# The MLP's first token block: its operands made tile pair by tile pair, or first half before second half

## Chip, cores and metric

The kernel runs on one core of a Trainium2 chip. The metric is device time in microseconds: the median of three runs of the kernel before is 1969.99 us (1968.49 to 1970.82). A profile of one execution goes with it.

## The reference

One decoder layer on 2048 tokens of 1024 features, float32 throughout. A mixer block (attention with a window of 128 and a short gated convolution, joined by an output projection) is followed by the MLP:

```python
x = x + y @ w_out[l]
hm = rms_norm(x, mlp_norm_g[l])
x = x + jnp.square(jax.nn.relu(hm @ w_up[l])) @ w_down[l]
```

`w_up` is 1024 x 4096, `w_down` 4096 x 1024.

## The kernel before

Each float32 product is made as three fast matmuls, on the high and the low parts of both operands (an ACT cast gives the high part, a DVE subtraction the low one). The mixers go through four chunks of 512 tokens. The MLP's up projection goes over two token blocks of 1024 tokens, and in each it is a two by two block product done with seven instead of eight products: the activations of a token block are cut into four blocks (feature half by token half), called b11, b21 (first 512 tokens) and b12, b22 (other 512 tokens), and seven operands are made of them. Operand 1 is b11, 2 is b21, 3 is b22, and 5, 6, 7, 4 are differences. The products are taken in the order of `ORDER`, 1, 2, 6, 5, 3, 7, 4; the first eight of them use operands 1 and 2 alone, for four groups of columns each.

**Making the operands of the first token block** is the job of `prepare_mlp` (L887 on), and this is what the change touches. A residual stream `x1` lies in DRAM, token by token. A tile pair (jj, i) holds 128 features of each feature half, jj of 0 to 3, for 512 tokens, i of 0 (first half) or 1 (other half). One step of the loop does this:

- DVE transposes (L313) two 128 x 512 halves of a fetched tile into blocks of `xs`, and scales each in place (L314). That is `turned`, two calls.
- SP fetches the tile pair two steps ahead: `load_turned`, four pieces (L307). The fetched tiles `xt` have two buffers, so the fetch of step n + 2 waits for the transposes of step n.
- For i = 0, two stores put the blocks into the operands 1 and 2 in DRAM (`x_put`, L318).
- For i = 1, `x_sums` does four differences (L324) and five stores (L318), in this order:

```python
x_put(tb, jj, 3, b22)
sub(5, t1, b12, b11)
sub(6, b11, b22, t1)
sub(7, b12, b22, b12)
sub(4, b21, b21, b11)
```

Each `sub` is a DVE subtraction and a store of its result; the second and the fourth overwrite b11 and b21, which were stored as operands 1 and 2. The blocks lie in two tiles `xs` of eight blocks each, which take the place of the normed activations of the last chunk (tags `h0`, `h1`), so the loop can't begin before the last chunk's projections are done with these.

The loop is a generator. `besides` (L918 on) takes one of its steps, then three groups of matmuls of the output projection, and so on; the output projection of the last chunk has a conv half (matmuls on `yt_c`) and an attention half (on `at_b`), each over two halves of the columns, and its evictions run on DVE (L872). After the last step and the rest of the conv half, `begin_mlp` emits what the MLP needs first: `load_x(0, 1)`, that is two SP loads of operand 1 from DRAM (L379) with a cast on ACT (L380) and a subtraction on DVE (L381), then four pieces of up weights (`wu_first`, L391) with their casts (L396, L397). Behind it come the output projection's last weights (`w_wo`, L235), then operand 2 and the loop over the products (matmuls at L1404).

What sets the order: the framework fixes each engine's list of instructions when the program is built, from the order in which the code emits them, shifts of priority (`ahead`, `PRIO`; zero for this loop) and its own estimate of when inputs and buffers are free. On the chip each engine, and SP's queue of DMA issues too, runs its list in order and waits at semaphores.

Of the kernel before, what the change touches and what calls it, by code (L numbers as in the profile page):

```python
# [50 lines left out]
NB = BW // P  # L51
# [51 lines left out]
def hymba_layer(  # L103
# [53 lines left out]
    def row(tag, name, bufs, dt=F32):  # L157

        return pool.tile([P, D], dt, tag=tag, name=name, bufs=bufs)
# [35 lines left out]
    def ahead(i):  # L195

        offset = PRIO[stage[0]][i]
        return tc.high_priority(offset=offset) if offset else nullcontext()
# [103 lines left out]
    def load_turned(xb, src, r0, jj):  # L302

        for pg in range(4):
            rows = src[r0 : r0 + BW].rearrange("(q i) (k c) -> i k q c", i=TS, k=2)
            c0 = jj * P + pg * TS
            nc.sync.dma_start(  # L307
                xb[pg * TS : (pg + 1) * TS].rearrange("p (k q c) -> p k q c", k=2, c=TS), rows[:, :, :, c0 : c0 + TS]
            )

    def turned(xb, k, dst, g, rs_row):

        nc.vector.transpose(dst, xb[:, k * BW : (k + 1) * BW])  # L313
        nc.vector.scalar_tensor_tensor(dst, dst, g, rs_row, op0=ALU.mult, op1=ALU.mult)  # L314

    def x_put(tb, jj, i, b):

        nc.sync.dma_start(xop_dram[tb][ORDER.index(i)][:, jj * BW : (jj + 1) * BW], b)  # L318

    def x_sums(tb, jj, b11, b21, b12, b22, t1):  # L320


        def sub(i, dst, a, b):
            nc.vector.tensor_tensor(dst, a, b, op=ALU.subtract)  # L324
            x_put(tb, jj, i, dst)
# [6 lines that stand above are left out]
# [192 lines left out]
    with tc.tile_pool(name="mix_small", bufs=1) as mix_small, tc.tile_pool(name="mix", bufs=1) as mix:  # L524
# [362 lines left out]
        def prepare_mlp():  # L887


            xs = [pool.tile([P, 8, CH], F32, tag=f"h{i}", name=f"xm{i}", bufs=1) for i in range(2)]  # L890
            rows = pool.tile([P, 2, BW], F32, tag="gb", name="rs_rows", bufs=1)
            for i in range(2):
                nc.sync.dma_start(rows[:, i], rs_dram[i].partition_broadcast(P))
            xts = {}

            def fetch(jj, i):
                xts[jj, i] = row("xt", f"xt_m{i}_{jj}", 2)
                load_turned(xts[jj, i], x1_dram, i * BW, jj)

            tiles = [(jj, i) for jj in range(NB) for i in range(2)]  # L900
            fetch(*tiles[0])
            fetch(*tiles[1])
            yield
            for n, (jj, i) in enumerate(tiles):
                bs = [xs[jj % 2][:, m] for m in range(5)]
                with ahead(9):
                    for k in range(2):
                        turned(xts[jj, i], k, bs[2 * i + k], g_cols[:, NB * k + jj : NB * k + jj + 1], rows[:, i])
                if n + 2 < len(tiles):
                    fetch(*tiles[n + 2])  # L910
                if i:
                    x_sums(0, jj, *bs)
                else:
                    x_put(0, jj, 1, bs[0])
                    x_put(0, jj, 2, bs[1])
                yield

        def besides(c, before, h, yt, rc, x1, h_next, z_next):  # L918
# [12 lines left out]
            if c + 1 < NCHUNK:  # L931
                h_next += parts(pool, "h", f"h{c + 1}")
                steps = prepare(xf, (c + 1) * CH, g_row[0], h_next, f"a{c + 1}")
            else:
                steps = prepare_mlp()
# [615 lines left out]
```

## Time and profile before

| | |
|---|---|
| profiled execution | 1970.88 us |
| its span | 1969.2 us |
| median of three runs | 1969.99 us |
| PE busy | 1916.1 us, 97% |
| DVE busy | 1212.6 us, 62% |
| ACT busy | 827.1 us, 42% |
| POOL busy | 275.0 us, 14% |
| HBM read, written | 284.78 MB, 125.84 MB |

The profile shows one execution, in us from its start. PE is the matmul engine, DVE the vector engine, ACT the scalar engine, POOL GpSimd, SP the engine whose queue issues most DMAs (SPq in rows). A timeline row has the start, the length, the engine, the line of the kernel, the operation, the tiles written and read, how many such instructions were merged, and in brackets the engine's idle time before it and what ended that. The length of a merged row reaches from the first start to the last end. A row of the chain of waits has start, length and who held the end at that time. A row of the windows has a stretch, its length, and for each engine the busy time and the number of instructions.

### The profile page before, as it was taken

To read this page: it belongs to the slowest core of one execution; us is meant where nothing else is said; L and a number is where in the kernel's file an instruction comes from. 1 tells how busy PE (TensorE), PEld (TensorE's weight loads), DVE (VectorE), ACT (ScalarE), POOL (GpSimd) and SP (SyncE) were. 2 spreads that over 40 slices of the span, in tenths; PEclk is the share of its full clock that TensorE was granted. 3 is DMA by queue.
4 is the path that set the end of the run, shared out by engine and by line. 5 is a ranking of instruction groups with operands and counts; after the bars stand their busy time and mean duration, and the time that the engine had idled before them with its cause. 6 is when DMAs were issued, how large, how long until landed. Compare 5 with 4: busy or idle time off the path is not lost.

```text
span 1969.2 us, 24719 instructions
## 1 busy us (share of the span) xinstructions
PE 1916.1 (97%) x8961; PEld 1595.4 (81%) x8961; DVE 1212.6 (62%) x1896; ACT 827.1 (42%) x1577; POOL 275.0 (14%) x475
## 2 busy tenths in 40 slices
PE   9999999999999949999999999999999999999999
PEld 8888877888888737788887888888888888888887
DVE  4885656448456857789879767666544334447441
ACT  6564444335434216445456545554332233232320
POOL 1122212312221101322201111011000000100000
PEclk9999999999999969999999999999999999999999
DMA  9774864564674588877876444437964456766641
GB/s 321 276 271 128 267 246 171 203 225 155 198 256 171 145 266 289 207 221 234 246 232 217 161 165 145 150 123 259 392 236 149 143 163 228 257 233 214 214 141 54
DMA packets 269387, 412.26 MB, mean 209 GB/s; under 512 B 84936, under 2 KB 174032, under 8 KB 257488
## 3 DMA queue, kind: packets, MB, share of 16 engines
q1 hardware_dynamic: 240512, 335.15, 51.8%
q0 software_dynamic: 15488, 51.40, 7.1%
q10 hardware_dynamic: 13264, 24.13, 3.3%
q8 instruction: 71, 1.16, 0.2%
q14 instruction: 52, 0.43, 0.1%
HBM read 284.78 MB, written 125.84 MB: 209 GB/s over the span
## 4 chain that ended last, share of the span: by engine, by line
PE 84%; issue 5%; DMA 5%; DVE 3%; POOL 2%; ACT 1%; SPq 1%; POOLq 0%; DVEq 0%; ACTq 0%
PE d L1511 31%; PE u L1404 24%; PE pout L266 2%; PE pout L267 2%; PE pout L268 2%; PE pz L266 2%; PE pz L267 2%; PE pz L268 2%; PE pc_c L268 1%; PE px_c L266 1%; PE px_c L268 1%; PE px_c L267 1%; PE pc_c L266 1%; PE pc_c L267 1%; PE psc_b L645 1%
## 5 line engine op out<-in xcount | busy, mean ns | idle before, releaser
L1404 PE MATMUL u<-op_x,wop 128*128 128x512 f32 x2688 | 620.5, 393 | 38.9 <-ACT wop L396 34.7
L1404 PEld LDWEIGHTS u<-op_x,wop 128*128 128x128 f32 x2688 | 509.3, 190 | 149.6 <-ACT wop L396 35.6
L1511 PE MATMUL d<-op_w,op_f 128*128 128x512 f32 x2688 | 609.4, 389 | 0.0
L1511 PEld LDWEIGHTS d<-op_w,op_f 128*128 128x128 f32 x2688 | 504.7, 188 | 104.6
L381 DVE TENSOR_TENSOR op_f<-op_f 128x1024 fp32r<-128x1024 f32 x112 | 136.8, 1224 | 233.5 <-ACT op_f L380 233.3
L380 ACT CAST op_f<-op_f 128x1024 fp32r<-128x1024 f32 x112 | 117.5, 1051 | 355.2 <-DMA op_f<-fop 352.2
L396 ACT CAST wop<-wu 128x512 fp32r<-128x512 f32 x156 | 96.2, 620 | 97.7 <-PE u L1404 92.3
L397 DVE TENSOR_TENSOR wop<-wu,wop 128x512 fp32r<-128x512 f32 x156 | 111.1, 713 | 37.4 <-DMA wu<-in_w_up_dram 20.1
L1140 POOL DMA_DIRECT2D fop<-s x96 | 52.1, 543 | 442.4 <-DVE s L1143 435.4
L1146 DVE TENSOR_TENSOR u<-u,u 128x512 f32<-128x512 f32 x128 | 87.6, 684 | 23.2 <-PE u L1404 23.2
L381 DVE TENSOR_TENSOR op_w<-raw,op_w 128x1024 fp32r<-128x1024 f32 x56 | 68.3, 1222 | 26.6 <-ACT op_w L380 26.6
L380 ACT CAST op_w<-raw 128x1024 fp32r<-128x1024 f32 x56 | 58.8, 1052 | 43.7 <-PE d L1511 20.3
L1152 ACT ACTIVATE u<-u 128x512 f32<-128x512 f32 x64 | 40.5, 632 | 54.2 <-DVE u L1146 52.3
L662 ACT ACTIVATE sc_b<-sc_b,ngm_b 128x128 f32<-128x128 f32 x128 | 49.6, 389 | 27.3 <-DVE ngm_b L659 27.3
L380 ACT CAST op_x<-op_x 128x1024 fp32r<-128x1024 f32 x28 | 29.2, 1047 | 72.3 <-DMA op_x<-xop 72.2
L694 POOL TENSOR_SCALAR_AFFINE_SELECT pp_b<-pp_b 128x512 fp32r<-128x512 f32 x60 | 41.2, 698 | 104.3 <-ACT pp_b L687 47.9
L1353 POOL DMA_DIRECT2D wds<-raw x16 | 8.5, 534 | 333.8 <-DVE raw L1351 333.8
L396 ACT CAST wop<-wu_s 128x512 fp32r<-128x512 f32 x64 | 39.4, 620 | 37.4 <-PE u L1404 30.1
L266 PE MATMUL pout<-w_wo,yt_c 128*128 128x512 f32 x128 | 52.0, 406 | 0.0
L268 PE MATMUL pout<-w_wo,yt_c 128*128 128x512 f32 x128 | 51.4, 402 | 0.0
L267 PE MATMUL pout<-w_wo,yt_c 128*128 128x512 f32 x128 | 50.7, 396 | 0.0
L266 PE MATMUL pout<-w_wo,at_b 128*128 128x512 f32 x128 | 50.1, 394 | 0.2 <-DVE x L872 0.2
(252 smaller groups left out, 3129.4 us busy)
## 6 DMA issues: line engine op xcount, KB each, us to landing
op_f<-fop SPq DMA_DIRECT2D x112, 512.0 KB, 4.4
raw<-in_w_down_dram SPq DMA_DIRECT2D x72, 512.0 KB, 4.4
wu<-in_w_up_dram SPq DMA_DIRECT2D x128, 256.0 KB, 4.0
w_wo<-wo SPq DMA_DIRECT2D x24, 1024.0 KB, 7.0
fop<-s POOLq DMA_DIRECT2D x96, 256.0 KB, 2.6
fop<-u ACTq DMA_DIRECT2D x64, 256.0 KB, 2.7
op_x<-xop SPq DMA_DIRECT2D x28, 512.0 KB, 7.8
w_q<-qkv SPq DMA_DIRECT2D x24, 512.0 KB, 6.0
```

The costliest lines, as they stand in the source:

```text
L266: nc.tensor.matmul(ps, st(0), mv(0), start=first, stop=False)
L267: nc.tensor.matmul(ps, st(0), mv(1), start=False, stop=False)
L268: nc.tensor.matmul(ps, st(1), mv(0), start=False, stop=last)
L380: nc.scalar.copy(op[:, 0], raw)
L381: nc.vector.tensor_tensor(op[:, 1], raw, op[:, 0].bitcast(F32), op=ALU.subtract)
L396: splits.append(nc.scalar.copy(hi, blk).ins)
L397: nc.vector.tensor_tensor(lo, blk, hi.bitcast(F32), op=ALU.subtract)
L662: nc.scalar.activation(sc[:, hd, :], sc[:, hd, :], AF.Exp, bias=ngm[:, hd : hd + 1], accum_out=den[:, hd : hd + 1])
L1140: eng.dma_start(fop_dram[tb][ORDER_DOWN.index(i)][n // 2][:, n % 2], b)
L1146: return nc.vector.tensor_tensor(dst, ps, b, op=ALU.add).ins
L1404: nc.tensor.matmul(pt, wops[i][:, a, k, :], xops[tb, p][k // 2][:, b, k % 2, :], start=p not in GOES_ON and k + j == 0, stop=k + j == NB + ...
L1511: nc.tensor.matmul(ps[tb][j], fs[tb][:, a, k, j * P : (j + 1) * P], w[:, b, k, :], start=first and p not in GOES_ON and k + n == 0, stop=l ...
```

## The change

The loop takes all four tile pairs of the first 512 tokens and then all four of the other 512, in place of taking the two in turn for each jj. The blocks of the first half now stay until the second loop: all eight lie in the first tile of `xs`. The second half's two blocks and the scratch block `t1` lie in the second tile, in two sets of three that are used in turn. What a step computes, fetches and stores is the same, and so are all shapes.

```diff
-            tiles = [(jj, i) for jj in range(NB) for i in range(2)]
+            tiles = [(jj, i) for i in range(2) for jj in range(NB)]
             fetch(*tiles[0])
             fetch(*tiles[1])
             yield
             for n, (jj, i) in enumerate(tiles):
-                bs = [xs[jj % 2][:, m] for m in range(5)]
+                bs = [xs[0][:, 2 * jj + k] for k in range(2)]
+                if i:
+                    bs += [xs[1][:, 4 * (jj % 2) + k] for k in range(3)]
                 with ahead(9):
                     for k in range(2):
                         turned(xts[jj, i], k, bs[2 * i + k], g_cols[:, NB * k + jj : NB * k + jj + 1], rows[:, i])
                 if n + 2 < len(tiles):
                     fetch(*tiles[n + 2])
                 if i:
                     x_sums(0, jj, *bs)
                 else:
                     x_put(0, jj, 1, bs[0])
                     x_put(0, jj, 2, bs[1])
                 yield
```

## The prediction

> **What bounds the kernel now.** I read the page first, then the windows by stretch around the one dip in its PE row, then the timelines of PE, SP and DVE there, and last the chain of waits across it.
>
> ```profile
> span 1969.2 us, 24719 instructions
> PE 1916.1 (97%) x8961; PEld 1595.4 (81%) x8961; DVE 1212.6 (62%) x1896; ACT 827.1 (42%) x1577; POOL 275.0 (14%) x475
> ```
> ```profile
> 660.00:680.00 20.00, 19.92 (x93) 16.05 (x92) 14.49 (x28) 4.75 (x8) 3.27 (x6) 1.00 0.52 134
> 680.00:700.00 20.00, 6.02 (x28) 4.69 (x26) 16.87 (x28) 0.00 (x0) 0.80 (x2) 0.73 0.71 163
> 700.00:720.00 20.00, 2.48 (x6) 1.78 (x7) 9.88 (x15) 4.38 (x6) 0.00 (x0) 0.50 1.04 326
> ```
> ```profile
> 685.63 0.39 PE L268 MATMUL pout<-w_wo,at_b 128*128 128x512 f32 x1
> 717.52 5.89 PE L1404 MATMUL u<-op_x,wop 128*128 128x512 f32 x13 [31.50 <-ACT wop L396]
> ...
> 736.64 21.92 PE L1404 MATMUL u<-op_x,wop 128*128 128x512 f32 x96
> ```
>
> PE is busy for 1916.1 of 1969.2 us, so the end moves by what PE's idle time changes. Of the 53 us that are idle, 31.5 lie in one place: PE is full up to 680 (19.92 of 20 us), ends the output projection at 686.0, and starts the MLP at 717.52. The changed loop runs in just this place. (The columns after the length are PE, PEld, DVE, ACT, POOL, the granted clock, the DMA share and GB/s.)
>
> Who holds PE is in the chain of waits and in SP's queue:
>
> ```profile
> 707.68 0.32 SPq L318
> 708.00 0.05 issue
> 708.09 0.41 SPq L379
> 708.60 7.24 DMA op_x<-xop
> 715.90 0.70 ACT op_x L380
> 716.61 0.25 issue
> 716.85 0.62 ACT wop L396
> ```
> ```profile
> 649.62 5.03 SPq L307 DMA_DIRECT2D xt_m<-x_dram  x4
> 654.69 1.14 SPq L318 DMA_DIRECT2D xop<-xm  x2
> 655.92 3.84 SPq L307 DMA_DIRECT2D xt_m<-x_dram  x4
> 659.87 11.16 SPq L318 DMA_DIRECT2D xop<-xm  x5
> 671.32 3.23 SPq L307 DMA_DIRECT2D xt_m<-x_dram  x4
> 674.60 2.29 SPq L318 DMA_DIRECT2D xop<-xm  x2
> 682.44 2.71 SPq L307 DMA_DIRECT2D xt_m<-x_dram  x4
> 685.25 5.03 SPq L318 DMA_DIRECT2D xop<-xm  x5
> 690.32 3.46 SPq L307 DMA_DIRECT2D xt_m<-x_dram  x4
> 693.83 1.13 SPq L318 DMA_DIRECT2D xop<-xm  x2
> 695.06 3.82 SPq L307 DMA_DIRECT2D xt_m<-x_dram  x4
> 698.98 9.01 SPq L318 DMA_DIRECT2D xop<-xm  x12
> 708.09 0.92 SPq L379 DMA_DIRECT2D op_x<-xop  x2
> 709.11 3.16 SPq L391 DMA_DIRECT2D wu_first<-in_w_up_dram  x4
> 712.32 4.05 SPq L235 DMA_DIRECT2D w_wo<-wo  x2
> 716.47 1.06 SPq L379 DMA_DIRECT2D op_x<-xop  x2
> ```
>
> Read downwards, SP's rows are the loop: four pieces of a tile pair fetched (L307), then two stores of a first half or five of a second half (L318), and only after the last store, issued at 707.68, the two loads of operand 1 (L379). From there it is 708.09 to 717.52, 9.4 us of load, cast and weight cast, to PE's first matmul. So **PE restarts 9.8 us after SP issues the loop's last store**, and the question is whether that point moves, or whether the loads come away from behind it.
>
> **The change, part by part.** The eight steps (a step is one tile pair) are regrouped. Before, steps 1, 3, 5, 7 have 4 DVE instructions (two transposes, two scalings) and 2 stores, and steps 2, 4, 6, 8 have 8 and 5 (four differences more, with five stores). After, steps 1 to 4 are the small ones, 5 to 8 the large ones. Nothing is added or removed: 48 DVE instructions, 28 stores, 32 fetches, the same shapes.
>
> *The order in SP's queue.* Operand 1 reads only stores of small steps, so its data are in DRAM after step 4 now. It gains only if its loads stand earlier in SP's queue, and that order is fixed when the program is built. Here the trace speaks:
>
> ```profile
> 674.51 0.39 PE L268 MATMUL pout<-w_wo,yt_c 128*128 128x512 f32 x1
> ```
> ```profile
> 503.71 8.65 SPq L307 DMA_DIRECT2D xt_m<-x_dram  x6
> ```
>
> Loads are let past earlier ones where the queue has room: six pieces of the first two fetches went at 503.71, far ahead of loads that the code emits before them. Yet from 649.62 to 716.47 SP's order is exactly the code's. The last output weights (L235 at 712.32) have their place free once the projection's conv half ends at 674.51, and the first up weights (L391 at 709.11) read an input; neither went ahead of any of the 12 pieces and 21 stores issued from then to the loop's end. So the order takes SP as full over the whole loop, in which a fetch or a store was always waiting. After the change the same number of them waits, with 20 of the 28 stores in the last four steps, so there is even more to issue at the end. I take the order as the code's again: operand 1 last. Price of this part: 0.
>
> *The work in front of the gap.* Six differences leave the stretch in which PE is busy. They were hidden beside full PE (19.92 of 20), so taking them away wins 0.
>
> *The work in the gap.* This is where they go. DVE in the gap:
>
> ```profile
> 686.50:708.00 21.50, 16.68 (x26) 0.56 0.93 266
> ```
> ```profile
> 686.79 1.29 DVE L313 STREAM_TRANSPOSE xm<-xt_m 128x512 f32<-128x512 f32 x2
> ...
> 696.58 1.30 DVE L313 STREAM_TRANSPOSE xm<-xt_m 128x512 f32<-128x512 f32 x2 [2.15 <-DMA xt_m<-x_dram]
> ...
> 701.60 1.30 DVE L313 STREAM_TRANSPOSE xm<-xt_m 128x512 f32<-128x512 f32 x2 [1.22 <-DMA xt_m<-x_dram]
> ...
> 706.21 1.44 DVE L324 TENSOR_TENSOR xm<-xm 128x512 f32<-128x512 f32 x2 [0.68 <-DMA xop<-xm]
> ```
> ```profile
> xop<-xm SPq DMA_DIRECT2D x28, 256.0 KB, 3.5
> xt_m<-x_dram SPq DMA_DIRECT2D x24, 128.0 KB, 3.8
> ```
>
> Step 5 starts at 686.79 behind the projection's last eviction and will start there again. Before, 26 of the loop's instructions are left then (x26; 2 differences of step 4, then 4, 8, 4, 8), 16.68 us, 0.64 each; they end at 707.65 because DVE also waits 2.15 + 1.22 + 0.68 = 4.05 us. After, 32 are left: 6 x 0.64 = 3.9 us more work. The three waits are what pays for it. The first two are fetches that stood behind five stores in SP's queue (685.25 before 690.32); the third is a difference that overwrites a block whose store had just been issued, and those stores are four steps old now.
>
> I lay the last four steps out with 8 x 0.64 = 5.13 us each: step 5 at 686.8, 6 at 691.9, 7 at 697.1, 8 at 702.2.
> - Step 7's fetch is issued when step 5's transposes end (688.1), with only two stores ahead of it, takes 3.46 us of SP, and its last piece lands 3.8 us after its issue, near 694.7: in time.
> - Step 5's five stores follow from 691.6 at about 0.6 us each (the seven from 698.98 take some 4 us), to 694.6; then step 8's fetch, 3.82 us, to 698.4, landed near 701.3: in time.
> - **The added wait** is on blocks. The second tile's two blocks and the scratch block come from a set that returns after two steps, not four. Step 7 needs step 5's fourth store landed: issued near 693.4, 3.5 us, 696.9: just in time. Step 8 needs step 6's fourth store, issued behind step 8's own fetch near 700.2, landed 703.7, where DVE is there at 702.2: **1.5 us**. Behind the waiting transpose on DVE stand only this step's own instructions; the last stores wait for them, and PE for those.
>
> The end is then 702.2 + 1.5 + 5.13 = 708.8, against 707.65: **1.2 us later**. The 9.8 us behind it stay, as the same loads follow.
>
> The landing of a store is the softest figure. The Trainium skill, page "DMA: Bandwidth & Descriptors", section "Anatomy of one DMA", puts a transfer at about 2.0 us plus bytes over 436 GB/s, an estimate of 2.6 us for 256 KB; by it step 8 would wait 0.6 us and the sum would be 0.3 us. The row's 3.5 us is at a DMA share of 0.93, so I keep it.
>
> **The sum.** The profiled execution took 1970.88 us, 1.7 more than its span, and is 0.9 above the median of 1969.99. 1969.99 + 1.2 = **1971.2 us**. About 0.2%, 3.9 us, is what a measurement of this kernel can tell from no change.
>
> **Rivals.**
> *A, the forecast: the stores move, the loads don't.* The change does not do what it says in time. For it: SP's order above. 1971.2, within 1 us below and 2.5 above.
>
> *B, operand 1's loads go ahead of the differences' stores.* That needs a moment in which the build sees SP without a waiting fetch or store after step 4. Step 4's two stores would follow the fetch of 682.44 from 685.2 to 686.4 and land 3.5 us later, 689.9; plus 9.4 us, PE starts at 699.3, 18.2 us earlier. It has work: 8 products of 12 matmuls on operands 1 and 2 (96 in 21.92 us) and the projection's last 48 (10.9 us at the same pace), some 33 us, while the differences, held up by 9.2 us of loads (0.92 + 3.16 + 4.05 + 1.06), end near 717 and operand 6 is ready near 727. So nothing is given back: 1970.0 - 18.2 = 1951.8. If the loads pass only the last step's five stores (about 4 us), 1966. Against it: neither ready load did so before.
>
> The matmuls after the gap run slowly, 13 in 5.89 us where 96 take 21.92 us: 2.9 us, with the granted clock at 0.50 in the stretch before. The page "TensorE: Matmul & The Clock Gate" of the Trainium skill, Part 1, has the clock halved after an idle window of about 3.4 us; by that rule a shorter gap of 13 us still costs these 2.9 us, so B is not worth more than 18.2.
>
> *C, slower: reuse after two steps decides.* Place: the first transposes of steps 7 and 8. If a store takes the 7.24 us of the load at 708.60, behind a full queue, step 7 waits until 693.4 + 7.2 = 700.6, 3.5 us, and step 8 until 707.4, where DVE arrives at 705.7, 1.7 us; the end is 712.5, 4.9 us later: 1974.9. With a landing of L the end is 700.2 + L + 5.13, so it decides from 6.2 us on. If the 4.05 us of waits stay too (the fetches late all the same), 1978. For it: the DMA share of 0.93. Against it: stores landed in 3.5 us at that very share.
>
> **How the numbers follow.** A 0.55, B 0.20 (0.10 whole, 0.10 in part), C 0.25. A lies within 0.2%, B is faster by over 0.2% (its smallest form sits at 4 us), C slower. The range leaves out the whole of B and the far end of C, about 0.16: 1962 to 1977.5. A alone: 1970.2 to 1973.7.
>
> **What would show it.** Right: SP's rows show 4, 2 four times, then 4, 5, 4, 5, 5, 5, and L379 behind the last L318; DVE runs 32 loop instructions from about 686.8 with under 2 us of waits; the fetch waits of 2.15 and 1.22 us are gone; a wait <-DMA xop<-xm stands before a transpose of step 8; PE's gap is 32 to 34 us. Wrong: L379 or L391 between L318 rows (B), or waits of over 2 us before the transposes of steps 7 and 8, or a later start than 686.8 (C). A shift in how PE mixes projection and MLP matmuls from 717 to 760 would be an effect that I have at nothing; its cover is that everything behind the last store is the same list.

## The result and the profile after

The changed kernel takes 1970.74 us (median of 20 runs, 1965.71 to 1975.53), the kernel before 1969.58 us (20 runs beside them, 1965.45 to 1971.42). The ratio is 1.0009, with a 95% interval of 1.0001 to 1.0017: 1.8 us slower, between 0.2 and 3.3. That is within the 0.2% of the forecast, which had +1.2 us. The profiled execution took 1968.23 us.

First the page of the changed kernel, its span and busy times:

```profile
span 1966.4 us, 24724 instructions
PE 1913.4 (97%) x8961; PEld 1592.7 (81%) x8961; DVE 1212.2 (62%) x1896; ACT 826.9 (42%) x1577; POOL 274.0 (14%) x475
```

PE idles 1966.4 - 1913.4 = 53.0 us; before it was 53.1. Now PE's timeline around the dip. (The MLP's matmuls, L1404 before, are L1406 here; the lines below L897 are as before.)

```profile
685.76 0.39 PE L268 MATMUL pout<-w_wo,at_b 128*128 128x512 f32 x1
717.56 5.97 PE L1406 MATMUL u<-op_x,wop 128*128 128x512 f32 x13 [31.41 <-ACT wop L396]
```

The gap is where it was, ends on the same cast, and is 31.41 us long, against 31.50. SP's queue beside it:

```profile
685.61 1.49 SPq L318 DMA_DIRECT2D xop<-xm  x2
...
691.50 2.66 SPq L318 DMA_DIRECT2D xop<-xm  x5
...
698.46 10.25 SPq L318 DMA_DIRECT2D xop<-xm  x15
708.80 0.91 SPq L379 DMA_DIRECT2D op_x<-xop  x2
709.81 2.98 SPq L391 DMA_DIRECT2D wu_first<-in_w_up_dram  x4
```

The stores moved: two behind the small step, then five, then 15 for the last three large steps. The loads of operand 1, whose last store is one of the two at 685.61, did not: they are issued at 708.80 behind all 28 stores, and the first up weights behind them, as before. DVE in the gap, steps 5 to 8:

```profile
686.93 1.29 DVE L313 STREAM_TRANSPOSE xm<-xt_m 128x512 f32<-128x512 f32 x2
...
691.97 1.30 DVE L313 STREAM_TRANSPOSE xm<-xt_m 128x512 f32<-128x512 f32 x2
...
697.01 0.70 DVE L313 STREAM_TRANSPOSE xm<-xt_m 128x512 f32<-128x512 f32 x1
...
702.48 0.70 DVE L313 STREAM_TRANSPOSE xm<-xt_m 128x512 f32<-128x512 f32 x1
703.22 0.75 DVE L314 SCALAR_TENSOR_TENSOR xm<-xm,g_cols,rs_rows 128x512 f32<-128x512 f32 x1
704.21 0.71 DVE L313 STREAM_TRANSPOSE xm<-xt_m 128x512 f32<-128x512 f32 x1 [0.24 <-DMA xop<-xm]
704.96 0.75 DVE L314 SCALAR_TENSOR_TENSOR xm<-xm,g_cols,rs_rows 128x512 f32<-128x512 f32 x1
...
706.47 1.89 DVE L324 TENSOR_TENSOR xm<-xm 128x512 f32<-128x512 f32 x3
```

The loop's instructions in that stretch, from the windows (the columns after the length are the busy time on DVE with the count, then clock, DMA share and GB/s):

```profile
686.50:709.00 22.50, 20.84 (x32) 0.56 0.97 285
```

There are 32, as laid out, and the waits of 2.15, 1.22 and 0.68 us are gone. Steps 5 and 6 take 5.04 us each, step 7 takes 5.47 and step 8 5.88. In steps 5 and 6 both transposes come first (x2), then both scalings. In steps 7 and 8, as the four rows from 702.48 show, DVE's list has one block's transpose and scaling, then the other's. These are the two steps whose blocks were used two steps before, and the block transposed second is the one that waits for a store in step 8 (0.24 us). That the build expected this block late and put ready work in front of it is my reading; the second experiment below bears it out. The last difference ends at 708.36, 22.60 us after PE's last projection matmul of 685.76; before it was 707.65 - 685.63 = 22.02. So the loop ends 0.58 us later, and from there to PE's first matmul it took 9.20 us instead of 9.87: in this execution the two cancel.

### The profile page after: what moved, and what is told of

Its sections match the earlier page's. It is cut to its first block, busy times and chain, and to the rows that moved or that the text cites. A ratio compares the mean times of both kernels' runs of the same rounds, so it can differ in the third digit from the quotient of the medians.

```text
span 1966.4 us, 24724 instructions
## 1 busy us (share of the span) xinstructions
PE 1913.4 (97%) x8961; PEld 1592.7 (81%) x8961; DVE 1212.2 (62%) x1896; ACT 826.9 (42%) x1577; POOL 274.0 (14%) x475
## 3 DMA queue, kind: packets, MB, share of 16 engines
q8 instruction: 71, 1.16, 0.2%
## 4 chain that ended last, share of the span: by engine, by line
PE 52%; issue 4%; DMA 1%; DVE 1%; POOL 1%; ACT 0%; POOLq 0%; SPq 0%; DVEq 0%
PE d L1513 31%; PE u L1406 21%; DMA fop<-s 0%; POOL fop L1142 0%; DVE wop L397 0%; DMA raw<-in_w_down_dram 0%; DMA op_f<-fop 0%; DMA xop<-st_m 0%; POOL st_m L1082 0%; DVE u L1148 0%; DVE op_x L381 0%; DVE wu L1124 0%; DVE s L1145 0%; DVE f L1145 0%; DVE st_m L313 0%
## 5 line engine op out<-in xcount | busy, mean ns | idle before, releaser
L1406 PE MATMUL u<-op_x,wop 128*128 128x512 f32 x2688 | 617.1, 392 | 39.4 <-ACT wop L396 33.3
L1406 PEld LDWEIGHTS u<-op_x,wop 128*128 128x128 f32 x2688 | 506.2, 189 | 149.7 <-ACT wop L396 34.3
```

What stands on the lines that cost most here:

```text
L1406: nc.tensor.matmul(pt, wops[i][:, a, k, :], xops[tb, p][k // 2][:, b, k % 2, :], start=p not in GOES_ON and k + j == 0, stop=k + j == NB + ...
```

## The experiments

My account was the prediction's: loads stay behind the stores, and the small loss is the reuse of the second tile's blocks. The rivals were that the loads can be freed and the regrouped loop then pays (B's price), and that reuse costs more than it shows (C). All ratios are against the kernel before on the same chip. The profiled executions are shifted against each other before the loop begins: the same loads of output weights (L235 or L236, x2), with 3222 matmuls done in each, are issued at 616.01 us in one execution and at 620.56 us in another. So where I compare times of two kernels below, I count from these loads or from PE's last projection matmul.

**The change again, and with blocks that are not reused so soon.** The first is the changed kernel unaltered; the second chooses the blocks so that the two that a large step transposes into were stored three steps ago or not at all.

```diff
-                    bs += [xs[1][:, 4 * (jj % 2) + k] for k in range(3)]
+                    bs += [xs[1][:, m] for m in ((0, 1, 2), (4, 5, 6), (3, 7, 2), (0, 1, 6))[jj]]
```

> The changed kernel once more, for a second profile and an interval. My account (the stores move, the queue's order and so operand 1's loads do not): PE's gap before the MLP is 31 to 33 us again, the last store is issued 0.5 to 1.5 us after 707.7, and the time is 0 to 2 us above before. Rival (the loss sits elsewhere, in a stage behind the gap): the gap is as before, and some other stretch of PE between 717 and 800 has 1 us or more of idle time more than before.

> The changed kernel with the five blocks of steps 7 and 8 laid so that none is taken back before its store has long landed (the two spare blocks of the second tile are used). My account, as the trace after has it: the reuse after two steps costs only about 0.3 us of waiting and some 0.9 us of a worse order on DVE (transpose, scaling, transpose, scaling with a gap before each scaling), so the last store is issued 1.0 to 1.4 us earlier than in the changed kernel and the time falls by about 1 us, to that of before. Rival (reuse is free, the loss is only run-to-run): no shift of the last store, under 0.3 us.

The change again: 1968.64 us, ratio 1.0012 (0.9998 to 1.0026), 2.2 us above before by the medians where I had 0 to 2. The loss does not sit behind the gap: there PE waits 6.55 us up to 900 us in the kernel before, 6.19 in the change and 6.43 in the change again. With other blocks: 1967.07 us, 0.9996 (0.9982 to 1.0009). PE of the change again, then of the other blocks:

```profile
683.61 0.39 PE L268 MATMUL pout<-w_wo,at_b 128*128 128x512 f32 x1
716.09 4.89 PE L1406 MATMUL u<-op_x,wop 128*128 128x512 f32 x13 [32.09 <-ACT wop L396]
```
```profile
683.55 0.39 PE L268 MATMUL pout<-w_wo,at_b 128*128 128x512 f32 x1
714.15 5.32 PE L1406 MATMUL u<-op_x,wop 128*128 128x512 f32 x13 [30.22 <-ACT wop L396]
```

And DVE with the other blocks, the first instructions of step 7 and the last differences:

```profile
694.79 1.29 DVE L313 STREAM_TRANSPOSE xm<-xt_m 128x512 f32<-128x512 f32 x2
696.01 1.37 DVE L314 SCALAR_TENSOR_TENSOR xm<-xm,g_cols,rs_rows 128x512 f32<-128x512 f32 x2
...
703.06 1.90 DVE L324 TENSOR_TENSOR xm<-xm 128x512 f32<-128x512 f32 x3
```

The old order is back, no step waits, every step takes 5.04 us, and the last difference ends 704.96 - 683.55 = 21.41 us after the last projection matmul. In the change it was 22.60 us and in the change again 704.45 + 1.89 - 683.61 = 22.73, so the loop ends 1.2 to 1.3 us earlier, as expected. The gap is 1.2 us shorter than in the change and 1.9 us shorter than in the change again; what goes beyond the 1.2 to 1.3 lies behind the loop. So the reuse is what the change costs in the gap, by the wait and by the order that the build makes of it. The intervals of the two times overlap, so the total shows it only in its direction (1.6 us between the medians, 0.16% between the ratios).

**The loads taken off SP's queue.** Operand 1's two loads and the four first up weights are issued by ACT, once in the changed kernel and once in the kernel before.

```diff
-        return [load_op(src[:, h], f"x{tb}_{p}_{h}", early=p in ORDER[:2]) for h in range(2)]
+        eng = nc.scalar if (tb, p) == (0, 1) else nc.sync
+        return [load_op(src[:, h], f"x{tb}_{p}_{h}", early=p in ORDER[:2], eng=eng) for h in range(2)]
...
-            load_up(b, m, 1, p)
+            load_up(b, m, 1, p, eng=nc.scalar)
```

> The changed kernel with the two loads of operand 1 and the four first up weights issued from ACT's queue in place of SP's; nothing else moved. My account (operand 1 is in DRAM after step 4 and only its place behind 20 stores in SP's queue holds it): the loads go at about 690, PE restarts near 700 in place of 717.5, and after some loss to the operand 2 and the output weights, which stay on SP, the time is 9 to 15 us below before, about 1958. Rival (the gap is held by something else, the transfers or DVE): PE restarts at 712 or later and the time is at most 4 us below before.

> The kernel before with the same six loads on ACT's queue. There operand 1 is whole only after step 7's stores, landed near 703.6. My account: PE restarts near 712, 5 us earlier, and the time is 4 to 7 us below before, so that the change of the loop is worth 5 to 10 us once the queue no longer holds it. Rival (the order of the loop does not matter even then): the same time as with the changed loop within 2 us.

The changed loop: 1965.06 us, 0.9986 (0.9973 to 1.0000), far short of the 9 to 15 us expected. The loop of before: 1961.21 us, 0.9973 (0.9961 to 0.9985). Its time is as expected, its account is not: PE starts at 692.03 on the operand's first half, and the changed loop is worth nothing beside it where I had 5 to 10 us. PE of the changed loop, every row that ends a wait from the gap to 900 us:

```profile
686.76 1.07 PE L1407 MATMUL u<-op_x,wop 128*128 128x512 f32 x4
688.97 4.83 PE L1407 MATMUL u<-op_x,wop 128*128 128x512 f32 x20 [1.14 <-DVE op_x L381]
696.70 1.22 PE L1407 MATMUL u<-op_x,wop 128*128 128x512 f32 x2 [2.90 <-ACT op_x L380]
700.18 6.72 PE L1407 MATMUL u<-op_x,wop 128*128 128x512 f32 x22 [2.27 <-DVE op_x L381]
719.50 1.65 PE L266 MATMUL pout<-w_wo,at_b 128*128 128x512 f32 x3 [12.59 <-DMA w_wo<-wo]
721.95 0.79 PE L267 MATMUL pout<-w_wo,at_b 128*128 128x512 f32 x1 [0.80 <-DMA w_wo<-wo]
736.32 2.59 PE L1407 MATMUL u<-op_x,wop 128*128 128x512 f32 x10 [0.99 <-DVE wop L398]
741.23 0.73 PE L1407 MATMUL u<-op_x,wop 128*128 128x512 f32 x2 [2.32 <-ACT wop L397]
742.50 13.44 PE L1407 MATMUL u<-op_x,wop 128*128 128x512 f32 x58 [0.54 <-ACT wop L397]
759.37 41.60 PE L1407 MATMUL u<-op_x,wop 128*128 128x512 f32 x182 [3.43 <-ACT wop L397]
803.67 3.06 PE L1407 MATMUL u<-op_x,wop 128*128 128x512 f32 x12 [2.70 <-DVE wop L398]
807.95 92.25 PE L1407 MATMUL u<-op_x,wop 128*128 128x512 f32 x405 [1.22 <-DVE wop L398]
```

The same of the loop of before:

```profile
692.03 8.28 PE L1405 MATMUL u<-op_x,wop 128*128 128x512 f32 x24 [5.25 <-ACT op_x L380]
715.55 4.19 PE L1405 MATMUL u<-op_x,wop 128*128 128x512 f32 x8 [15.23 <-ACT op_x L380]
...
738.40 0.73 PE L1405 MATMUL u<-op_x,wop 128*128 128x512 f32 x2 [0.59 <-ACT wop L397]
739.79 13.44 PE L1405 MATMUL u<-op_x,wop 128*128 128x512 f32 x58 [0.66 <-ACT wop L397]
755.82 41.60 PE L1405 MATMUL u<-op_x,wop 128*128 128x512 f32 x182 [2.59 <-ACT wop L397]
800.15 100.07 PE L1405 MATMUL u<-op_x,wop 128*128 128x512 f32 x427 [2.73 <-DVE wop L398]
```

Read the brackets. With the changed loop PE goes into operand 1 without a pause at 686.76 and does 48 matmuls of it in the old gap. Then it stands 12.59 us for the output weights, which are still behind the stores, and later 0.99 + 2.32 + 0.54 + 3.43 us for weight casts. All its waits add up to 30.9 us. The loop of before gets only 24 matmuls into the gap, but stands 0.59 + 0.66 + 2.59 us for weight casts there; its waits add up to 27.1 us. The 3.9 us between the sums stand beside 3.85 us between the medians and 0.13%, 2.6 us, between the ratios, whose intervals overlap. (After the change as it was, the sum up to 900 us was 37.6, before 38.1.) So the earlier operand is real, and is lost to what comes next in the queues.

**Operand 2 and the output weights taken along.** The same edit, with `(tb, p) in ((0, 1), (0, 2))` and the output weights of the last chunk (`wo01`) on ACT's queue too.

> The changed loop with operand 1, operand 2, the first up weights and the output projection's last weights all loaded from ACT's queue. After e3, where PE stood 12.6 us for the output weights on SP, my account is that each of these loads was held by its place behind the stores alone: PE runs the projection's last 48 matmuls and the four products on operand 1 from 687 to about 712, then waits for the next up weights, which stay on SP (about 722). Time 10 to 16 us below before. Rival (the transfers or the vector engine hold the stretch, so loads moved forward only push the stores back): at most 4 us below before, as in e3.

> The loop of before with the same loads on ACT's queue. Operand 1's second half is there only near 709, but PE has the projection's 48 matmuls and the first half of the products to fill the time, and both loops then wait for the same up weights on SP. My account: 9 to 15 us below before, and within 3 us of e5. Rival (the order of the loop decides once the queue is free): 6 us or more slower than e5.

The changed loop: 1958.32 us, 0.9962 (0.9948 to 0.9976), short of what I expected. The loop of before: 1951.87 us, 0.9934 (0.9912 to 0.9956), the lowest median here and faster than both kernels of the case. I had expected the two within 3 us; by the ratios they are 0.28%, 5.5 us, apart, and the intervals just overlap. DVE in the changed loop, at the projection's end:

```profile
697.31 0.75 DVE L874 SCALAR_TENSOR_TENSOR x<-pout,ra,x 128x512 f32<-128x512 f32 x1 [1.97 <-PE pout L269]
697.98 1.29 DVE L314 STREAM_TRANSPOSE xm<-xt_m 128x512 f32<-128x512 f32 x2
```

Now that PE has the projection's last part to do in the gap, its evictions stand in front of step 5 on DVE, which begins 11 us later than in the change. The last differences end at 725.30 with the changed loop and at 717.45 with the loop of before, where six fewer differences are left behind that eviction. Counted from the output weights' loads, at 619.72 and 616.01, that is 105.58 and 101.44 us, 4.1 us apart. What follows: freeing the loads moves the loop's own end back, and then the work per step in the gap counts. But the waits of PE don't settle the pair: up to 900 us they add up to 23.3 us with the changed loop and 24.5 with the loop of before. Of the 6.0 us between the profiled spans, 3.7 were there before the loop began (619.72 - 616.01), so this pair of traces shows 2.3 us for all that follows. Whether the loop of before is really ahead here, and why, stays open.

**The stores taken off SP's queue.** The 28 stores are issued by POOL.

```diff
-        nc.sync.dma_start(xop_dram[tb][ORDER.index(i)][:, jj * BW : (jj + 1) * BW], b)
+        eng = nc.sync if tb else nc.gpsimd
+        eng.dma_start(xop_dram[tb][ORDER.index(i)][:, jj * BW : (jj + 1) * BW], b)
```

> The changed loop with its 28 stores issued from POOL's queue, the loads left on SP and not moved in the code. My account of the order (SP's list was full of stores and fetches, so nothing could go ahead): now the loads stand right behind the last fetch, near 698, before the last stores; PE restarts near 707, and the time is 6 to 12 us below before. Rival (the place of the loads in the list is not what holds them): PE restarts at 716 or later, within 2 us of before.

> The loop of before with its stores on POOL's queue. Operand 1 needs a store of step 7 (landed near 704), and SP waits for it with the load, so PE restarts near 712: 3 to 7 us below before, and 3 to 6 us slower than e7. Rival (as e7's): within 2 us of before.

The changed loop: 1961.78 us, 0.9986 (0.9974 to 0.9997), less than expected. The loop of before: 1960.05 us, 0.9980 (0.9967 to 0.9993), a gain in the range expected; but I had it 3 to 6 us slower than the changed loop, and the two can't be told apart. SP's queue with the changed loop:

```profile
680.40 16.83 SPq L307 DMA_DIRECT2D xt_m<-x_dram  x12
697.39 2.92 SPq L380 DMA_DIRECT2D op_x<-xop  x2
```

Without the stores in SP's list, the very same code has the loads right behind the last fetch, 9.3 us earlier than in the change when counted from the start of PE's gap (684.05 here, 686.15 there). So it was the loop's issues on SP that held them, as the prediction read it. Yet PE restarts only at 710.84: the gap is 26.79 us, 4.6 shorter. The other half of the 9.3 us goes between the loads' issue and PE's start, 13.45 us here and 8.76 in the change. Operand 1's loads took a median of 9.0 us to land and the first up weights 10.2, against 6.2 and 7.3 us in the change; here the loop's stores still run beside them.

**One set of blocks.** All four large steps use the same three blocks, so steps 6, 7 and 8 must each wait for the stores of the step before: reuse at its worst.

```diff
-                    bs += [xs[1][:, 4 * (jj % 2) + k] for k in range(3)]
+                    bs += [xs[1][:, k] for k in range(3)]
```

> The changed loop with one set of three blocks for all of steps 5 to 8, so that each of the steps 6, 7 and 8 takes back the blocks of the step just ahead: the suspected wait made larger and three times. My account: each of them waits until the fourth store of the step ahead has landed, about 0.6 us after its last difference for the issue, up to 3.8 us for a fetch ahead in SP's queue and 3.5 us for the landing, so 4 to 6 us a step; the last store is 12 to 17 us later, PE's gap 43 to 49 us, the time 11 to 17 us above before. Rival (a store's block is free as soon as it is issued, so reuse costs next to nothing): under 3 us.

Measured: 1966.66 us, 1.0007 (0.9994 to 1.0020). I had expected 11 to 17 us above before and missed that by 10 us, though the waits came. DVE:

```profile
693.34 0.71 DVE L313 STREAM_TRANSPOSE xm<-xt_m 128x512 f32<-128x512 f32 x1 [2.98 <-DMA xop<-xm]
...
696.37 0.71 DVE L313 STREAM_TRANSPOSE xm<-xt_m 128x512 f32<-128x512 f32 x1 [1.54 <-DMA xop<-xm]
...
706.42 0.71 DVE L313 STREAM_TRANSPOSE xm<-xt_m 128x512 f32<-128x512 f32 x1 [3.51 <-DMA xop<-xm]
```

SP of the same kernel shows why they cost nothing that the time shows:

```profile
689.65 2.84 SPq L318 DMA_DIRECT2D xop<-xm  x5
692.58 0.51 SPq L379 DMA_DIRECT2D op_x<-xop  x1
...
700.04 3.22 SPq L318 DMA_DIRECT2D xop<-xm  x5
703.36 0.41 SPq L379 DMA_DIRECT2D op_x<-xop  x1
703.87 0.43 SPq L391 DMA_DIRECT2D wu_first<-in_w_up_dram  x1
...
715.73 3.38 SPq L318 DMA_DIRECT2D xop<-xm  x4
```

The waits leave SP with nothing of the loop to issue, and the build puts operand 1's loads and the first weights into these holes, between the stores. That is rival B's picture, brought about by C's waits: the last stores are issued some 12 us later than in the change (counted from the start of PE's gap, and as I had expected), the gap of PE is 26.30 us, 5 shorter, and the two nearly cancel. (All of PE's waits up to 900 us add up to 35.4 us, against 37.6 in the change.)

**Both queues.** The kernel before with the stores on POOL and operands 1 and 2, the first up weights and the output weights on ACT's queue.

> The loop of before, stores on POOL's queue and operands 1 and 2, first weights and output weights on ACT's (e6 and e8 together). In e6 PE still stood 15.3 us for operand 1's second half, whose store is that of step 7; that does not move, but the next up weights no longer stand behind the stores. My account (the end of the loop on DVE holds what is left): within 4 us of e6, 10 to 17 us below before. Rival (SP's queue still held e6): 18 us or more below before.

Measured: 1956.96 us, 0.9954 (0.9938 to 0.9969). That is 8 to 9 us below before, where I had expected 10 to 17. By the ratios it is 0.2%, 4 us, short of the version without the POOL part, where I had expected the two within 4 us; the intervals overlap. In DVE's list the casts' subtractions now come ahead of the loop's last step:

```profile
718.70 2.53 DVE L383 TENSOR_TENSOR op_x<-op_x 128x1024 fp32r<-128x1024 f32 x2 [10.80 <-ACT op_x L382]
721.14 1.30 DVE L314 STREAM_TRANSPOSE xm<-xt_m 128x512 f32<-128x512 f32 x2
```

Step 8 waits 10.80 us for a load that isn't its own. A freer queue let the build put the operand in front, and an engine that runs its list in order paid for it.

## Why the prediction was right, step by step

- *PE's gap bounds the place.* Held. The gap is 31.41 us and in the second profile of the change 32.09; I had put 32 to 34, so the first lies below it.
- *SP's order is the code's; operand 1 stays last.* Held, and it decided. The order's reason was argued from two loads that did not move; the runs now show it. With the stores elsewhere, or with holes between them, the loads do go ahead.
- *The work taken out of the stretch before the gap is worth nothing.* Held as far as the gap shows: step 5 begins at 686.93, 1.17 us after the last projection matmul starts, before 686.79 - 685.63 = 1.16.
- *32 instructions, paid by three waits.* Held. Without a wait a step takes 5.04 us, where I had 5.13: 0.36 us less over four steps.
- *The added wait of 1.5 us at step 8.* Here the form was wrong and the sum nearly right. The store landed 0.5 us later than I put it: I had it issued at 700.2 and landed at 703.7; it was issued at 700.73, and the wait ends at 704.21. The time from issue to landing is the one I took:

```profile
xop<-xm SPq DMA_DIRECT2D x22, 256.0 KB, 3.6
```

  That is the DMA issues' row of the changed kernel for 686 to 709 us (the last number is the median from issue to landing). The estimate of 2.6 us that I had set beside it from the Trainium skill ("DMA: Bandwidth & Descriptors", "Anatomy of one DMA") is 1 us less. That section gives its fit for DMAs that GpSimd issues, which I had not said; these stores are SP's, at a DMA share of 0.97. Where the trace agrees with it is the MLP's 96 stores of 256 KB that POOL issues (`fop<-s`): they land in a median of 2.7 us. The loop's own stores, issued by POOL in the experiment above, took a median of 5.2 us (22 of them, from 675 to 720 us). But DVE did not stand still for the store: it ran the other block's transpose and scaling first, waited 0.24 us, and lost the rest by taking transposes and scalings in turn. Steps 7 and 8 together take 0.43 + 0.84 = 1.27 us more than 2 x 5.04. I had let only the step's own work stand behind the wait, and had not seen that this work can change places with it.
- *The end 1.2 us later.* Measured 0.58. From the prediction's 708.83 - 707.65 = 1.18, take 0.36 for the shorter steps and 0.23 for 1.27 in place of 1.5; that leaves 0.59. *The 9.8 us behind it stay*: 9.20, 9.75 and 9.19 us in three profiles (the change, the change again, the other blocks), so this stretch varies by as much as the effect.
- The +1.8 us of the medians isn't found in a row of the profiled execution, whose gap is as long as before. Its interval, 0.2 to 3.3, holds the 0.58 and the 1.2; more can't be said. That the forecast's +1.2 lies so near to +1.8 is in part luck, as the runs of the change alone spread over nearly 10 us.
- *Rival B* did not come, and its price was wrong where it could be tried. "Nothing is given back" fails: with the loads free, the changed loop gained 2.8, 7.5 and 2.8 us against the kernel before (ratios 0.9986, 0.9962, 0.9986), not 18.2. I had left out that the output weights and operand 2 stand behind the same stores, that weight casts then come late, and that operand 1 is loaded in two halves, the first of which needs only two of the four pairs, so that the old loop too has it early.
- *Rival C* did not decide: the stores landed in a median of 3.6 us, far from the 6.2 from which it would have decided, and step 8 waited 0.24 us. Even one set of blocks, with 8 us of waits, did not make the kernel measurably slower, though there the loads moved too. (The far end of C, 1974.9 + 4.05, comes to 1979, not to the 1978 of the prediction.)

## What to carry to other kernels

Having data ready earlier is worth nothing while the load that fetches them stands behind the rest of the loop in one in-order queue. Look first at where the consumer's load sits; here moving loads to another queue, in the loop as it was, gave 0.66% (0.44 to 0.88), and the reordering was never faster than the loop as it was. Once a load is free, add up all waits behind it up to where the two traces agree again, since the next loads, the casts and the loop's own end each took a part back. Compare the two traces from a point that both reach before the change, as here they were up to 4.55 us apart at such a point.

## What was not expected of the hardware and its build

- The reuse is hardly seen as a wait: beside the bracket's 0.24 us it cost 1.0 us over two steps by another instruction order.
- With the stores on POOL, the row of twelve fetch pieces on SP is 16.83 us long. In it SP waited 4.6 us for transposes, so the pieces took 12.2 us, 1.0 each. In the change, four at a time between stores, they took 2.94 to 4.12 us, 0.7 to 1.0 each. So issuing a fetch was no quicker with the stores on another queue.
- The spread of one kernel's runs is far larger than the effect: 1965.71 to 1975.53 us over 20 runs of the change. In the profiled executions up to 4.55 us of such a spread was there before the loop began.
